# Three moves in a hybrid decoder layer: the samples' mask load, the splits before the SSD branch projection, and the evictions of the output projection

## The chip, the cores and the metric

One core of a Trainium2 chip runs the whole program in one launch. The metric is device time in microseconds (us) of that core. Engines are named as in the profile: PE is TensorE's matmul, PEld its weight load, DVE is VectorE, ACT ScalarE, POOL GpSimd, and SP (SyncE) issues most transfers. L12 is line 12 of the kernel before.

## The reference, cut to what matters

One layer is computed for two groups that share the weights: a prompt of 256 tokens and 8 samples of 8 tokens, each with 2048 cached positions. Together they are 320 columns.

```
x = x + 0.5 * SwiGLU1(RMSNorm(x))
h = RMSNorm(x); P = h @ w_in_proj            # z, xBC, dt | q, k/v x 3, gates | merge gates
y_ssd = mamba_mixer(...)                     # conv, chunked scan, SiLU(z) gate, group norm of 4 x 512
y_nsa = sparse attention over compressed, selected and window rows of the cache
m = sig(gA) * (y_ssd @ w_branch_ssm) + sig(gB) * (y_nsa @ w_branch_attn)
x = x + m @ w_out
x = x + 0.5 * SwiGLU2(RMSNorm(x))
```

In the samples' window branch the 8 new keys of a sample are masked: key n is hidden from a query at t < n. That mask is the input wm, 128 x 8 numbers.

## The kernel before, in words

**Dense units.** All big products run through `dense` (L335). A unit is one output tile of 128 rows and 320 columns. Weights come from DRAM in blocks of 128 x 1024 f32 (512 KB) through three raw buffers. Each block is split into a high half `wh`, cast on ACT (`w_hi`, L317), and a lower half `wl`, a subtraction on DVE (`w_lo`, L326). The input is split the same way into `xh` and `xl`, by `split`: a cast on ACT (L261), then a subtraction on DVE (L264). For each of the k tiles PE runs three matmuls (L345 to L347), wh with xh, wh with xl, wl with xh, so 24 a unit at 8 tiles. Splitting is two units ahead of PE: at the start of a unit `w_hi` is issued for the unit two further on, after the third k tile `w_lo`, and `w_lo` ends by asking SP for the next raw block (L308), which waits until this DVE instruction has freed its buffer. wh and wl have three buffers each, the PSUM tiles of the units (tag pd) three.

**Side work.** Everything that is not a dense unit is written as generators in a scheduler S. After each k tile `S.tick()` runs: callbacks given to `S.defer(n, f)` fire after 2n ticks, then the generators get a step whenever a credit, filled at a rate set for each stage, reaches one. `S.step()` takes one step by hand. Engines work in order, and each queue holds its instructions as the program issues them.

**The samples' side work.** `ssd()` runs two generators mixed: `prompt_chunks` and `sample_chunks`. The first ends by taking `early_bias(2)`, a generator that loads the bias table in 16 pieces of 64 KB on SP, two a step (L1440), and, in a last step of its own, the mask `wb` (L1444); then `early_kv`, which loads the first three key/value tiles. A tile is four pages of 256 KB, two issued by SP and two by POOL (L1431), or one 1 MB window read by SP (L1427). `sample_attn` follows. Its first DVE instruction adds a part of the bias to the mask (L1458), so it needs both. Then it asks for four more tiles (a ring of seven, one of them in the tail of `xbc`) and goes through 40 tiles. One step transposes one tile's weights on PE (L1512; copied by ACT, L1514), in three steps of five computes scores for one or two tiles ahead (PE L1481 and L1486, maxima on DVE L1494, exponentials on ACT L1505), multiplies with the values (L1526), and does a part of the combine (L1541 to L1572). A tile is asked for, by a deferral of two ticks, after the step that used the tile seven before it. During this the dense units are those of z (L2016, L2017 gate them; squares and their sums for the group norm, L368, L373, L396) and then of the SSD branch.

**The SSD branch.** For each half h of the 16 input tiles, a loop splits eight tiles of xbc into yh and yl; then `NST` = 2 steps are taken by hand; then eight units follow.

**The output projection.** For each of eight units m: the eviction adds half of the product to x2 on DVE (L2073), scales it by the norm's weights (L416, DVE), splits that into hh and hl (L261, L264), squares x2 on ACT (L368) and gathers the squares on POOL, the last on DVE (L373). FFN 2 (`ffn`) then takes hh and hl as its input; its first unit needs all eight of them, in order.

```
for k in range(8):                                   # SSD branch, each half
    split(yh[:, k, :], yl[:, k, :], xbc[:, 8 * h + k, :])
for _ in range(NST):
    S.step()
for m in range(8):                                   # output projection
    p = bank("pd", (128, NT))
    dense(wo[m], mh, ml, p)
    v.scalar_tensor_tensor(x2[:, m, :], p, 0.5, x2[:, m, :], op0=ALU.mult, op1=ALU.add)
    norm_pre(x2, m, P_N2, hh, hl)
    sq.add(x2[:, m, :])
```

Of the kernel before, what the change touches and what calls it, by code (L numbers as in the profile page):

```python
# [10 lines left out]
F32 = mybir.dt.float32  # L11
# [4 lines left out]
ALU = mybir.AluOpType  # L16
# [22 lines left out]
P_N1, P_NM, P_N2, P_CW, P_CB, P_SN, P_DS, P_QN, P_DTB, P_AL, P_PE, P_W2, P_QR = (  # L39
    0, 8, 16, 24, 120, 144, 160, 176, 180, 181, 182, 214, 342)  # L40
# [67 lines left out]
NST = 2  # L108
# [89 lines left out]
def step_kernel(ctx, tc, I, O):  # L198
    nc = tc.nc
    pe, v, a, g, sp = nc.tensor, nc.vector, nc.scalar, nc.gpsimd, nc.sync  # L200
    ctx.enter_context(tc.manual_schedule())
    S = Sched()
# [8 lines left out]
    def bank(tag, shape=(128, 512)):  # L211
        bufs = dict(pd=3, sc=2, pt=2, po=1)[tag]
        t = ps.tile([128, 512], F32, tag=tag, bufs=bufs, name=f"ps_{tag}")[: shape[0], : int(np.prod(shape[1:]))]
        if len(shape) == 3:
            t = t.rearrange("p (a b) -> p a b", a=shape[1])
        elif len(shape) == 4:
            t = t.rearrange("p (a b c) -> p a b c", a=shape[1], b=shape[2])
        return t
# [39 lines left out]
    def split(hi, lo, src, eh="a"):  # L258

        if eh == "a":  # L260
            a.copy(hi, src)  # L261
        else:
            gcopy(hi, src)
        v.tensor_tensor(lo, src, hi, op=ALU.subtract)  # L264
# [35 lines left out]
    st = dict(load=0, split=0, raw={}, hl={})  # L300
# [34 lines left out]
    def dense(unit, xh, xl, out, cut=1, extra=None):  # L335

        k0, K = 0, sum(n for _, n in unit)
        for i, n in unit:
            w_ready(i + SA - 1)
            wh, wl = st["hl"].pop(i)  # L340
            w_hi()
            for k in range(n):
                s = slice(128 * k, 128 * k + 128)
                kk = k0 + k
                pe.matmul(out, wh[:, s], xh[:, kk, :], start=kk == 0, stop=False)  # L345
                pe.matmul(out, wh[:, s], xl[:, kk, :], start=False, stop=False)  # L346
                pe.matmul(out, wl[:, s], xh[:, kk, :], start=False, stop=kk == K - 1)  # L347
                if extra:
                    extra()
                if k == 2:  # L350
                    w_lo()
                if (kk + 1) % cut == 0:
                    S.tick()
            k0 += n
# [58 lines left out]
    def norm_pre(x, k, gcol, hh, hl):  # L413

        h = tp.tile([128, NT], F32, tag="hf", name="hf")
        v.tensor_scalar(h, x[:, k, :], par[:, gcol + k : gcol + k + 1], None, op0=ALU.mult)  # L416
        split(hh[:, k, :], hl[:, k, :], h)

    def norm_scale(sq, pool):

        rsb = pool.tile([128, NT], F32, name="rsb")
        rs = tp.tile([128, 3], F32, tag="nrs", bufs=1, name="nrs")

        def spread():
            bc = bank("pt", (128, NT))
            spread_rows(bc, rs)
            a.copy(rsb, bc)

        S.defer(sq.delay + 1, lambda: sq.roots(rs))
        S.defer(sq.delay + 6, spread)  # L430
        return rsb
# [351 lines left out]
    hh = hp_.tile([128, 8, NT], F32R, tag="hh", name="hh")  # L783
    hl = hp_.tile([128, 8, NT], F32R, tag="hl", name="hl")
# [16 lines left out]
    sq = Squares(8, 6)  # L801
# [4 lines left out]
    sq = Squares(8)  # L806
# [11 lines left out]
    hh = hp_.tile([128, 8, NT], F32R, tag="hh", name="hh")  # L818
    hl = hp_.tile([128, 8, NT], F32R, tag="hl", name="hl")
# [613 lines left out]
    def early_bias(n):  # L1433
        pl = right.enter_context(tc.tile_pool(name="sb", bufs=1, side="right"))
        st["bias"] = pl.tile([128, PAST], F32, name="bias")
        for i in range(2 * T):
            t, s = divmod(i, 2)
            src = bass.AP(tensor=tr0.tensor, offset=tr0.offset + (16 * TL + 512) * s + 7 - t,
                          ap=[[TL, 16], [1024, 2], [1, 512]])
            sp.dma_start(st["bias"][t :: T, :].rearrange("p (c s n) -> p c s n", c=2, s=2)[:, :, s, :], src)  # L1440
            if i % n == n - 1:
                yield
        st["wb"] = pl.tile([128, 8], F32, name="wb")
        sp.dma_start(st["wb"], I["wm"])  # L1444
        yield

    def early_kv():
        pl = right.enter_context(tc.tile_pool(name="sk", bufs=1, side="right"))
# [167 lines left out]
    def ssd():  # L1616
# [118 lines left out]
        def prompt_chunks():  # L1735
# [9 lines left out]
            for i, (q, c) in enumerate(items):  # L1745
                if i + 1 < 8:
                    if c:
                        yield from until(("x", q + 1))
                    stage_a(*items[i + 1])
                yield  # L1750
                if i + 1 < 8:
                    decay(*items[i + 1])
                stage_b(q, c)
                yield
                if i + 2 < 8:
                    load_ab(*items[i + 2])
                state(q, c)
                if c:
                    ready["y", q] += 1
                if i + 1 < 8:  # L1760
                    weigh(*items[i + 1])
                if c and q < 3:
                    load_ecb(q + 1)
                yield
                store("outS")
                if i == EB:
                    yield from until("conv")
                    late = early_bias(2)
                if i >= EB:
                    next(late, None)  # L1770
# [149 lines left out]
    p = bank("pd", (128, NT))  # L1920
# [12 lines left out]
    for i in range(12):  # L1933
        p = bank("pd", (128, NT))
# [11 lines left out]
    for i in range(4):  # L1946
        p = bank("pd", (128, NT))
# [14 lines left out]
    for i in range(4):  # L1962
        p = bank("pd", (128, NT))
# [12 lines left out]
    for n, i in enumerate(XBC_RUN):  # L1976
        p = bank("pd", (128, NT))
# [14 lines left out]
    for i in range(16):  # L1992
        p = bank("pd", (128, NT))
# [32 lines left out]
    for i in range(16):  # L2026
        if i % 4 == 0:
            force(lambda: ready["y", i // 4] == 2)
            sq = Squares(4, fold=True)
        p = bank("pd", (128, NT))  # L2030
# [3 lines left out]
    for h in range(2):  # L2034
        if h:
            S.flush()
        yh = hp_.tile([128, 8, NT], F32R, tag="hh", name="yh")
        yl = hp_.tile([128, 8, NT], F32R, tag="hl", name="yl")
        for k in range(8):
            split(yh[:, k, :], yl[:, k, :], xbc[:, 8 * h + k, :])  # L2040
        for _ in range(NST):
            S.step()
        for m in range(8):
            p = bank("pd", (128, NT))
            dense(wbs[h][m], yh, yl, p)
            if h == 0:
                a.copy(xbc[:, m, :], p)
            else:
                v.tensor_tensor(xbc[:, m, :], xbc[:, m, :], p, op=ALU.add)
                v.scalar_tensor_tensor(mg[:, m, :], mg[:, m, :], 1.0, xbc[:, m, :], op0=ALU.add, op1=ALU.mult)  # L2050
# [4 lines left out]
    so, x2, oh_, ol_ = (st[k] for k in ("so", "x2", "oh", "ol"))  # L2055
    mhl = hp_.tile([128, 16, NT], F32R, tag="Ax", name="mhl")
    mh, ml = mhl[:, 0:8, :], mhl[:, 8:16, :]
    for m in range(8):
        p = bank("pd", (128, NT))
# [7 lines left out]
    sq = Squares(8, 5, True)  # L2067
    hh = hp_.tile([128, 8, NT], F32R, tag="hh", name="hh")
    hl = hp_.tile([128, 8, NT], F32R, tag="hl", name="hl")
    for m in range(8):  # L2070
        p = bank("pd", (128, NT))
        dense(wo[m], mh, ml, p)
        v.scalar_tensor_tensor(x2[:, m, :], p, 0.5, x2[:, m, :], op0=ALU.mult, op1=ALU.add)  # L2073
        norm_pre(x2, m, P_N2, hh, hl)
        sq.add(x2[:, m, :])
    rsb = norm_scale(sq, so)

    def evac2(m, p):
# [155 lines left out]
```

## Time and profile before

| | |
|---|---|
| median of 3 runs (lowest, highest) | 1316.9 us (1314.0, 1320.02) |
| the profiled execution | 1319.28 us |
| its span, first to last instruction | 1317.6 us |
| mean granted TensorE clock | 0.981 of 2.4 GHz |
| busy: PE, PEld, DVE, ACT, POOL | 96%, 87%, 67%, 45%, 26% |
| transfers | 251.67 MB, mean 191 GB/s |

Times inside the profile count from the first instruction. A busy PE is one with matmuls in flight, whatever its clock; PEclk is the clock that was granted, 1.00 for 2.4 GHz and 0.50 for 1.2 GHz, and a stretch with both shows a mean. The releaser in square brackets of a row is inferred; an engine named there that had long been done stands for another, often a transfer.

### The profile page before, as it was taken

To read this page: it belongs to the slowest core of one execution; us is meant where nothing else is said; L and a number is where in the kernel's file an instruction comes from. 1 tells how busy PE (TensorE), PEld (TensorE's weight loads), DVE (VectorE), ACT (ScalarE), POOL (GpSimd) and SP (SyncE) were. 2 spreads that over 40 slices of the span, in tenths; PEclk is the share of its full clock that TensorE was granted. 3 is DMA by queue.
4 is the path that set the end of the run, shared out by engine and by line. 5 is a ranking of instruction groups with operands and counts; after the bars stand their busy time and mean duration, and the time that the engine had idled before them with its cause. 6 is when DMAs were issued, how large, how long until landed. Compare 5 with 4: busy or idle time off the path is not lost. (4 is left out here: it accounts for less than half of the span.)

```text
span 1317.6 us, 28585 instructions
## 1 busy us (share of the span) xinstructions
PE 1260.2 (96%) x10779; PEld 1151.3 (87%) x10779; DVE 877.1 (67%) x1872; ACT 590.5 (45%) x1149; POOL 347.0 (26%) x567
## 2 busy tenths in 40 slices
PE   8999999999999998889999998898999999999998
PEld 8999999999988888777897777775769999999998
DVE  5576666655586577976568888777678665656542
ACT  4444444444455334446664442455564343333322
POOL 2233221232200335655335664121210010000000
PEclk9899999999999998999999999898999999999999
DMA  8466666766663445521167876998974444444553
GB/s 275 146 215 213 206 197 197 233 202 221 203 195 121 138 147 212 189 69 50 65 207 236 269 228 194 325 339 289 331 284 154 152 145 135 146 154 150 153 163 92
DMA packets 102212, 251.67 MB, mean 191 GB/s; under 512 B 14648, under 2 KB 41273, under 8 KB 100121
## 3 DMA queue, kind: packets, MB, share of 16 engines
q1 hardware_dynamic: 89722, 213.44, 49.1%
q0 software_dynamic: 12352, 36.40, 8.4%
q8 instruction: 85, 1.39, 0.4%
q14 instruction: 53, 0.43, 0.1%
HBM read 235.07 MB, written 23.10 MB: 196 GB/s over the span
## 5 line engine op out<-in xcount | busy, mean ns | idle before, releaser
L345 PE MATMUL ps_pd<-hh,wh 128*128 128x320 f32 x1320 | 440.9, 334 | 2.9 <-ACT hh L261 1.8
L326 DVE TENSOR_TENSOR wl<-wraw,wh 128x1024 fp32r<-128x1024 f32 (+1 forms) x245 | 303.2, 1239 | 178.0 <-ACT wh L317 172.2
L346 PE MATMUL ps_pd<-hl,wh 128*128 128x320 f32 x1320 | 413.8, 314 | 1.3 <-DVE hl L454 1.1
L347 PE MATMUL ps_pd<-hh,wl 128*128 128x320 f32 x1320 | 413.7, 313 | 1.2 <-DVE wl L326 1.1
L317 ACT CAST wh<-wraw 128x1024 fp32r<-128x1024 f32 (+1 forms) x245 | 252.1, 1031 | 139.1 <-PE ps_pd L346 99.8
L345 PEld LDWEIGHTS ps_pd<-hh,wh 128*128 128x128 f32 x1320 | 253.2, 192 | 22.0 <-issue 11.4
L346 PEld LDWEIGHTS ps_pd<-hl,wh 128*128 128x128 f32 x1320 | 253.6, 192 | 9.5 <-issue 4.8
L347 PEld LDWEIGHTS ps_pd<-hh,wl 128*128 128x128 f32 x1320 | 253.0, 192 | 2.0 <-DVE wl L326 2.0
L345 PE MATMUL ps_pd<-ah,wh 128*128 128x320 f32 x352 | 109.4, 311 | 0.0
L347 PE MATMUL ps_pd<-ah,wl 128*128 128x320 f32 x352 | 108.9, 309 | 0.0
L580 DVE TENSOR_TENSOR pgl<-pg,pgh 128x512 fp32r<-128x512 f32 x128 | 82.5, 685 | 29.6 <-ACT pgh L573 29.3
L346 PE MATMUL ps_pd<-al,wh 128*128 128x320 f32 x320 | 98.8, 309 | 0.0
L568 POOL DMA_DIRECT2D pg<-in_cache x136 | 74.2, 546 | 83.6 <-DVE pgl L580 42.3
L238 POOL TENSOR_SCALAR ah<-ff 128x320 fp32r<-128x320 f32 x44 | 20.1, 457 | 275.0 <-DVE ff L482 275.0
L477 ACT ACTIVATE sg<-sg 128x320 f32<-128x320 f32 x44 | 20.8, 472 | 127.1 <-DVE sg L476 127.1
L573 ACT CAST pgh<-pg 128x512 fp32r<-128x512 f32 x128 | 72.7, 616 | 10.0 <-PE ps_sc L714 8.0
L713 PE MATMUL ps_sc<-pgh,w1h 128*128 128x256 f32 x256 | 68.5, 288 | 1.3 <-ACT pgh L573 1.3
L714 PE MATMUL ps_sc<-pgh,w1l 128*128 128x256 f32 x256 | 68.2, 288 | 0.0
L345 PEld LDWEIGHTS ps_pd<-ah,wh 128*128 128x128 f32 x352 | 66.2, 188 | 0.4
L347 PEld LDWEIGHTS ps_pd<-ah,wl 128*128 128x128 f32 x352 | 66.1, 188 | 0.0
L346 PEld LDWEIGHTS ps_pd<-al,wh 128*128 128x128 f32 x320 | 60.2, 188 | 0.0
L1431 POOL DMA_DIRECT2D KV<-in_cache x54 | 29.1, 539 | 109.4 <-PE ps_po L1526 90.6
(476 smaller groups left out, 2207.5 us busy)
## 6 DMA issues: line engine op xcount, KB each, us to landing
wraw<-in_wproj SPq DMA_DIRECT2D x77, 512.0 KB
wraw<-in_w1in SPq DMA_DIRECT2D x44, 512.0 KB
wraw<-in_w2in SPq DMA_DIRECT2D x44, 512.0 KB
pg<-in_cache POOLq DMA_DIRECT2D x136, 128.0 KB, 4.0
pg<-in_cache SPq DMA_DIRECT2D x120, 128.0 KB
KV<-in_cache POOLq DMA_DIRECT2D x54, 256.0 KB, 5.9
KV<-in_cache SPq DMA_DIRECT2D x54, 256.0 KB
wraw<-in_w1out SPq DMA_DIRECT2D x16, 512.0 KB
```

Of the source, the lines that this page charges most:

```text
L317: a.copy(h[:, :n], st["raw"][i][:, :n])
L326: v.tensor_tensor(l[:, :n], st["raw"].pop(i)[:, :n], st["hl"][i][0][:, :n], op=ALU.subtract)
L345: pe.matmul(out, wh[:, s], xh[:, kk, :], start=kk == 0, stop=False)
L346: pe.matmul(out, wh[:, s], xl[:, kk, :], start=False, stop=False)
L347: pe.matmul(out, wl[:, s], xh[:, kk, :], start=False, stop=kk == K - 1)
L477: a.activation(s, s, AF.Silu)
L568: e.dma_start(page(s, half)[:, i, :], I["cache"][ds(r, 1), :, 256 * c : 256 * c + 256].rearrange("o p f -> p (o f)"))
L573: a.copy(h[:, 8 * half : 8 * half + 8, :], page(s, half)[:, :, 64 * q : 64 * q + 64])
L580: v.tensor_tensor(l[:, 8 * half : 8 * half + 8, :], page(s, half)[:, :, 64 * q : 64 * q + 64], h[:, 8 * half : 8 * half + 8, :], op=ALU.su ...
L713: pe.matmul(ph, wh[:, j, :], h[:, :, j, :], start=q + j == 0, stop=False)
L714: pe.matmul(ph, wl[:, j, :], h[:, :, j, :], start=False, stop=False)
L1431: e.dma_start(t[:, j, :], I["cache"][ds(r, 1), :, 512:1024].rearrange("o p f -> p (o f)"))
```

## The change

Three edits. `early_bias` asks for the mask first, ahead of all bias pieces and in the same step as the first two, and has no step of its own for it any more. In the SSD branch the two steps by hand are taken after the second and after the fifth of the eight splits. In the output projection the evictions of units 0 to 6 are deferred by three ticks, to the third k tile of the next unit, behind that tile's `w_lo`; the last one stays where it is.

```diff
     def early_bias(n):
         pl = right.enter_context(tc.tile_pool(name="sb", bufs=1, side="right"))
         st["bias"] = pl.tile([128, PAST], F32, name="bias")
+        st["wb"] = pl.tile([128, 8], F32, name="wb")
+        sp.dma_start(st["wb"], I["wm"])
         for i in range(2 * T):
...
             if i % n == n - 1:
                 yield
-        st["wb"] = pl.tile([128, 8], F32, name="wb")
-        sp.dma_start(st["wb"], I["wm"])
-        yield
...
         for k in range(8):
             split(yh[:, k, :], yl[:, k, :], xbc[:, 8 * h + k, :])
-        for _ in range(NST):
-            S.step()
+            if k in (1, 4):
+                S.step()
...
         dense(wo[m], mh, ml, p)
-        v.scalar_tensor_tensor(x2[:, m, :], p, 0.5, x2[:, m, :], op0=ALU.mult, op1=ALU.add)
-        norm_pre(x2, m, P_N2, hh, hl)
-        sq.add(x2[:, m, :])
+
+        def evac(m=m, p=p):
+            v.scalar_tensor_tensor(x2[:, m, :], p, 0.5, x2[:, m, :], op0=ALU.mult, op1=ALU.add)
+            norm_pre(x2, m, P_N2, hh, hl)
+            sq.add(x2[:, m, :])
+
+        if m < 7:
+            S.defer(1.5, evac)
+        else:
+            evac()
```

## Rows read from the trace of the kernel before

**Rows 1.** The page's first part: busy time, share of the span and instructions of each engine.

```profile
PE 1260.2 (96%) x10779; PEld 1151.3 (87%) x10779; DVE 877.1 (67%) x1872; ACT 590.5 (45%) x1149; POOL 347.0 (26%) x567
```

**Rows 2.** PE's waits between 795 and 1100 us: the waiting instruction, its inferred releaser, us in total, times, longest.

```profile
PE ps_pt L396 <- DVE ncol L401: 3.6, 1, 3.6
PE ps_sc L1481 <- DVE yl L264: 3.1, 2, 2.5
PE ps_sc L1838 <- DVE h L1840: 2.3, 1, 2.3
PE ps_sc L1481 <- DMA KV<-in_cache: 2.3, 2, 1.2
PE ps_pd L345 <- ACT hh L261: 1.8, 1, 1.8
```

**Rows 3.** Windows: the stretch in us, its length, busy us of each engine (instructions), granted clock, DMA share, GB/s.

```profile
800.00:810.00 10.00, 7.66 (x35) 5.47 (x34) 8.92 (x12) 1.84 (x3) 4.82 (x5) 0.83 0.54 184
...
835.00:840.00 5.00, 5.00 (x20) 4.97 (x21) 3.31 (x17) 0.14 (x2) 2.00 (x4) 0.50 1.05 404
840.00:845.00 5.00, 5.00 (x47) 2.04 (x46) 2.57 (x7) 1.94 (x5) 0.00 (x0) 0.92 1.01 395
930.00:940.00 10.00, 8.91 (x122) 5.41 (x114) 6.45 (x26) 4.18 (x10) 2.15 (x4) 1.00 0.85 280
1080.00:1090.00 10.00, 9.19 (x51) 8.94 (x52) 6.86 (x21) 3.77 (x5) 0.00 (x0) 0.83 0.48 158
845.00:985.00 140.00, 134.45 (x1974) 95.60 (x1976) 98.60 (x373) 81.02 (x186) 27.96 (x52) 0.98 0.88 314
```

**Rows 4.** SP's queue in order of time: start, us of issue, transfer, how many.

```profile
822.40 1.18 SPq L1440 DMA_DIRECT2D bias<-trev  x2
823.63 0.85 SPq L1444 DMA_DIRECT2D wb<-in_wm  x1
824.58 1.69 SPq L308 DMA_DIRECT2D wraw<-in_wproj  x1
...
827.85 4.75 SPq L1431 DMA_DIRECT2D KV<-in_cache  x6
```

**Rows 5.** The chain of work that ended last, in order of time: start, us, what. The last bias piece's issue and the mask's transfer.

```profile
822.99 0.59 SPq L1440
...
823.63 8.43 DMA wb<-in_wm
```

**Rows 6.** DVE in order of time: start, us, line, operation, shapes, how many; in brackets the idle time before it and its releaser.

```profile
832.14 0.17 DVE L1458 TENSOR_TENSOR wb<-wb,bias 128x8 f32<-128x8 f32 x1 [3.01 <-DMA wb<-in_wm]
...
833.15 1.22 DVE L326 TENSOR_TENSOR wl<-wraw,wh 128x1024 fp32r<-128x1024 f32 x1
834.28 0.48 DVE L373 TENSOR_TENSOR sqa<-sqa,sq 128x320 f32<-128x320 f32 x1
```

**Rows 7.** ACT in order of time: the high half before that lower half.

```profile
830.22 1.05 ACT L317 CAST wh<-wraw 128x1024 fp32r<-128x1024 f32 x1 [1.73 <-DMA wraw<-in_wproj]
```

**Rows 8.** PE in order of time, at the first half's splits: the scores of two tiles, and the first matmul of the branch.

```profile
900.93 1.02 PE L1481 MATMUL ps_sc<-xbc,qbs 64*32 64x512 f32 x2 [2.53 <-DVE yl L264]
903.19 1.03 PE L1481 MATMUL ps_sc<-KV,qbs 64*32 64x512 f32 x1 [1.24 <-DMA KV<-in_cache]
...
907.05 0.64 PE L345 MATMUL ps_pd<-yh,wh 128*128 128x320 f32 x1
```

**Rows 9.** SP's queue: the issue of the tile that lies in xbc.

```profile
893.00 0.92 SPq L1431 DMA_DIRECT2D xbc<-in_cache  x2
```

**Rows 10.** DVE there: the first of the second step's two maxima, and the last instruction of its combine.

```profile
905.72 0.69 DVE L1494 CUSTOM_DVE_ANT_0 P<-ps_sc,bias 128x512 f32<-128x512 f32 x1 [3.02 <-PE ps_sc L1486]
...
908.04 1.06 DVE L1572 TENSOR_REDUCE ocs<-R 128x64 f32<-128x512 f32 x1
```

**Rows 11.** ACT there: the second step's last exponential.

```profile
908.23 0.71 ACT L1505 ACTIVATE P<-P,ms 128x512 f32<-128x512 f32 x1
```

**Rows 12.** DVE in the output projection: lower half, the first eviction, its lower half of hl, the next unit's lower half; and the last eviction.

```profile
1050.91 1.23 DVE L326 TENSOR_TENSOR wl<-wraw,wh 128x1024 fp32r<-128x1024 f32 x1 [0.46 <-ACT wh L317]
1052.05 0.48 DVE L2073 SCALAR_TENSOR_TENSOR x<-ps_pd,x 128x320 f32<-128x320 f32 x1
...
1053.48 0.49 DVE L264 TENSOR_TENSOR hl<-hf,hh 128x320 fp32r<-128x320 f32 x1 [0.53 <-ACT hh L261]
1054.79 1.22 DVE L326 TENSOR_TENSOR wl<-wraw,wh 128x1024 fp32r<-128x1024 f32 x1 [0.82 <-ACT wh L317]
...
1079.25 0.48 DVE L2073 SCALAR_TENSOR_TENSOR x<-ps_pd,x 128x320 f32<-128x320 f32 x1
```

**Rows 13.** ACT there: the first eviction's cast, and the next high half.

```profile
1052.99 0.46 ACT L261 CAST hh<-hf 128x320 fp32r<-128x320 f32 x1 [2.11 <-DVE hf L416]
...
1053.73 1.03 ACT L317 CAST wh<-wraw 128x1024 fp32r<-128x1024 f32 x1
```

**Rows 14.** PE at the start of FFN 2: the wait for the last hh, and two matmuls in a row.

```profile
1080.70 0.41 PE L345 MATMUL ps_pd<-hh,wh 128*128 128x320 f32 x1 [1.82 <-ACT hh L261]
...
1081.62 0.31 PE L345 MATMUL ps_pd<-hh,wh 128*128 128x320 f32 x1
1081.77 0.31 PE L346 MATMUL ps_pd<-hl,wh 128*128 128x320 f32 x1
```

## The prediction

> **What bounds the kernel now.** The first view is busy time by engine: TensorE (PE) is busy 96% of the span [rows 1]. So the end moves only if PE's idle time shrinks, if its clock sits at 1.2 GHz for less time, or if new waits are put before it. The second view is PE's waits in the stretch that holds all three edits [rows 2]. The five longest come to 13 us: 3.6 us for a sum of squares, 3.1 us (2.5 and 0.6) at the samples' scores put down to the split (yl), 2.3 us (1.2 and 1.1) there for KV tiles, 1.8 us for hh at the start of FFN 2, and 2.3 us for h, which no edit touches. The third view is the windows [rows 3]. After the 2.3 us wait for h the clock averages 0.83 over 10 us, which is 10 x 0.17 x 2 = 3.4 us at 1.2 GHz. After the 3.6 us wait it is 0.50 for 5 us and 0.92 for the next 5, 5 + 0.8 = 5.8 us at least. After the 1.8 us wait it is 0.83 over 10 us, 3.4 us. Around the KV wait of 1.1 us it stays at 1.00. Half-rate time t costs t/2 of PE's work, so a long wait costs more than its idle time.
>
> The profiled execution took 1319.28 us (span 1317.6, 1.7 around it); the median of the three runs is 1316.9, 2.4 below it. I work out a gain against the first and take it off the median. A measurement of this kernel can tell about 0.5% (6.6 us) from no change.
>
> **Edit 1, the mask.** SyncE (SP) issues the last pair of bias pieces at 822.40 and the mask at 823.63 [rows 4]. The mask is only 4 KB, but it lands 8.43 us later, because it queues behind all that was issued before it [rows 5]. DVE's L1458 needs it and the bias, and stands idle 3.01 us until 832.14 [rows 6]. Everything on DVE behind L1458 is late by as much: the gating of the z unit, the weights' lower half at 833.15, and at 834.28 the sum for which PE waits. With the mask asked for ahead of all bias pieces, what is late next? First the bias: its last piece is issued 0.64 us ahead of the mask (822.99 to 823.63) on the same queue [rows 5]. If it takes as long, DVE gains 0.64; if it has landed by the time DVE arrives, the full 3.01. Second the weights: ACT's high half waits for its own transfer and starts at 830.22 [rows 7]. It ends at 831.3, and the lower half follows it, so at most 833.15 - 831.3 = 1.85 us is gained. L1458 also comes a step earlier in DVE's order and may now wait ahead of one gather like that at 834.28, 0.48 us, which takes the lower bound to 0.2. Bounds 0.2 to 1.85; I take 1.4, nearer the upper, since the bias pieces are ahead of the mask's 128 tiny packets.
>
> PE then resumes at 833.5 instead of 834.9, an idle time of 2.2 instead of 3.6. The nearest wait is the one of 2.3 us, with 3.4 us at half rate. Before, PE did 5.9 / 2 = 2.95 us of full-rate work from 834.9 to 840.8. Now it does 1.7 in 3.4 us and the other 1.25 at full rate, done at 838.15: gain 2.65. If the half-rate time stays as long, the gain is the bare 1.4. I take 2.6 for the edit.
>
> What it costs: one mask issue (0.85 us) stands ahead of the first bias pair, and what covers it is that nothing reads the bias before L1458, eight steps later: nothing, and 0.85 us for SP's weight loads without that cover. The generator also has one step fewer. So the three early KV loads, each two SP and two POOL transfers, come a step earlier. POOL has nothing else in its queue there. On SP the first one's SP half (512 KB) now stands ahead of the weight load at 824.58. Six such transfers take SP 4.75 us to issue [rows 4], so this load leaves 2 x 0.79 - 0.85 = 0.7 us later, with 512 KB ahead of it: at 395 to 404 GB/s [rows 3] another 1.3 us. It feeds a split that DVE reaches a dense unit later, 3.5 us of PE's work. With that cover the price is nothing; without it, 2 us.
>
> All sample steps also run one step earlier against the dense units, so at each split it is the next tile's step that falls there. That can move KV waits either way; the nearest rows are those waits themselves, 2.5 and 1.2 us [rows 8]. Price 0, bounds -3.7 to +3.7.
>
> **Edit 2, the splits.** No PE instruction lies among the eight splits; the steps' matmuls come after them in PE's order already. The wait at 900.93 is put down to yl, yet the score matmul L1481 reads a KV tile (kept in xbc) and qbs, not yl [rows 8]. SP issued that tile at 893.00 to 893.92 [rows 9], so it would have landed after 7.0 us, against 8.43 for the mask. I read 900.93 as a landing, and the next wait, 903.19, is named as one. So moving steps between splits takes off nothing: the scores wait for KV in either order. It can cost: the splits left for after the second step now stand behind its maxima and its combine on DVE (905.72 to 909.1) [rows 10] and its exponentials on ACT (to 908.9) [rows 11]. PE starts the first unit at 907.05 and wants split 5 after fifteen matmuls of 0.147 us, 2.2 us at full rate, so at 909.3; splits come every 0.4 us from about 909.2 with lower halves 0.5 later. Price 0.3 us for both halves together; bounds -0.5 (ACT's transposed copies start earlier) and +2.
>
> **Edit 3, the output projection.** DVE and ACT run one loop per unit: lower half 1050.91, eviction 1052.05, next lower half 1054.79 [rows 12]; cast 1052.99, and behind it and the square the next high half 1053.73 [rows 13]. The period is 3.88 us, where PE needs 24 matmuls of 0.147 us (1081.62 to 1081.77) [rows 14], 3.53. So the evictions fall behind by 0.35 a unit, and the last one (1079.25) makes PE wait for hh. Putting eviction m behind the split of unit m+1 does not break this loop: the order around it, high half, lower half, eviction, cast, square, high half, is the same, and ACT must still pass each cast before the next high half. It saves only the first eviction's place, where two splits now run back to back: high half 1 as soon as PE has left unit 0 (about 1051.1, where 1053.73 stood), lower half 1 at 1052.1 behind lower half 0, eviction 0 at 1053.3, high half 2 at 1055.0, and from there 3.88 a unit: high half 7 at 1074.4, eviction 6 at 1074.4 + 1.06 + 1.14 = 1076.6. Eviction 7 follows it directly on DVE, behind its lower half (1053.48 + 0.49 - 1052.05 = 1.9): 1078.45 instead of 1079.25. Gain 0.8; bounds 0 (the loop slips back) and 1.8 (no wait left). hh then comes at 1079.9, not 1080.70. The wait shrinks from 1.8 to about 1.05, nearest to that of 1.1 which left the clock at full. So I also take off half of the 3.4 us at half rate, 1.7. Edit 3: 2.5, or 0.8 if the clock drops all the same.
>
> **Sum.** 2.6 - 0.3 + 2.5 = 4.8 us: 1314.5 for the profiled execution, 1312.1 for the median.
>
> **A rule against it.** The mask's row shows 8.43 us in a busy queue [rows 5]. The Trainium skill, "DMA: Bandwidth & Descriptors", section "Anatomy of one DMA — SWDGE (gpsimd) path", fits a transfer (of the other issuing path) as some 2 us plus its bytes over the peak rate. By that the mask was in place before DVE asked and the wait was for something else: edit 1 is worth nothing and the sum is 2.2. The row speaks against it here; it is the third rival.
>
> **Rivals.**
> 1. Forecast, 0.42: gains of 3 to 7 us.
> 2. Given back to KV, 0.20. The stage of the samples runs with DMA at 0.88 of its time [rows 3], and PE stands there for tiles. If the landings at 903 and 938 don't move, the 2.6 of edit 1 turns into longer waits: 1314.7. For: both waits. Against: KV loads are released by PE's own progress, so they should shift with it.
> 3. The mask was not the last to come, 0.10. The bias, or another transfer, holds L1458 as long: 1314.7 too, by edit 3 alone.
> 4. The step shift helps, 0.20. The scores fall in the first of the two steps at the split with their tiles asked for a step sooner; some 2.5 of the 3.7 us goes, and 1.7 of half rate: 1312.1 - 4.2 = 1308.
> 5. Slower, 0.08: the late splits starve PE. If the tiles are in time, PE reaches the first unit straight away, while splits wait for maxima and exponentials (two of 0.7 us each) that wait for PE's scores. That is some 3 us at each half, plus 1.7 of clock: 2 x 4.7 = 9.4, so 1312.1 + 9.4 = 1321.5. It decides once a half loses over 2.4 us, and passes 0.5% only if edit 1 fails as well.
>
> **Numbers.** Likeliest 1312.1. Range 1307 to 1318.5: below, rival 4 with the longer DVE gain; above, no gain and part of rival 5. Under 1310.3 lie rival 4 and a little of the forecast, 0.26; over 1323.5 the tail of rival 5, 0.04; 0.70 within.
>
> **What would show it.** Right: L1458 idle about 1.5 us or less and not on the mask; PE's wait for the sum about 2.2; half rate after it shorter; eviction period still 3.88 in the middle, the last one at about 0.8 us nearer to its unit; the wait for hh near 1 us and the clock at 1.00 after it; score waits at the splits still there. Wrong: a period of 3.5, no DVE wait at L1458 at all, or a score wait at the split that vanishes with KV landing as before.

## The result: 0.54% slower, lost among the samples' key/value tiles

| | before | after |
|---|---|---|
| median | 1318.55 us (8 runs) | 1326.6 us (8 runs) |
| profiled execution, its span | 1319.28, 1317.6 us | 1328.19, 1326.5 us |
| ratio, 95% interval | | 1.0054 [1.0032, 1.0076] |

On 1318.5 us the ratio is +7.1 us, interval 4.2 to 10.0. The forecast was a gain of 4.8 us, and no rival came as high: the slowest stood at 1321.5. Busy time and PE's waits from 795 to 1110 us, as in [rows 1, 2]; lines behind the diff have moved by one or two, so L1480 is the scores (L1481 before):

```profile
PE 1269.7 (96%) x10779; PEld 1155.8 (87%) x10779; DVE 877.7 (66%) x1872; ACT 590.1 (44%) x1149; POOL 346.7 (26%) x567
```

```profile
PE ps_sc L1480 <- DMA KV<-in_cache: 6.6, 3, 3.6
PE ps_pt L396 <- DVE sqa L373: 3.1, 2, 2.1
...
PE ps_sc L1480 <- DMA KV<-in_cwin: 1.7, 1, 1.7
PE ps_pt L396 <- DVE ncol L401: 1.6, 1, 1.6
PE ps_sc L1480 <- DMA xbc<-in_cache: 1.5, 1, 1.5
PE ps_pd L345 <- ACT hh L261: 1.0, 1, 1.0
```

Over the whole span PE is idle as long as before (1326.5 - 1269.7 = 56.8 us, and 57.4), but busy 9.5 us longer with the same instructions, at a mean granted clock of 0.976 for 0.981. So part of the loss is clock, as the stages below show.

The two waits that edits 1 and 3 aimed at shrank: the sum (ncol) from 3.6 to 1.6, hh from 1.8 to 1.0. Larger are the score waits on tiles, 6.6 + 1.7 + 1.5 = 9.8 us in five waits, where before had 5.4 with those put down to yl, and the wait for sqa, 3.1 for 1.0. PE's rows show where the shorter sum, four of the five tile waits and the longer wait for sqa lie (start, us, idle before and its releaser):

```profile
831.77 0.78 PE L396 MATMUL ps_pt<-ones,sqa 128*128 128x1 f32 x6 [1.64 <-DVE ncol L401]
884.14 1.85 PE L1480 MATMUL ps_sc<-KV,qbs 64*32 64x512 f32 x14 [3.58 <-DMA KV<-in_cache]
914.67 0.94 PE L396 MATMUL ps_pt<-ones,sqa 128*128 128x1 f32 x6 [2.10 <-DVE sqa L373]
952.23 1.06 PE L1480 MATMUL ps_sc<-KV,qbs 64*32 64x512 f32 x8 [1.69 <-DMA KV<-in_cwin]
958.70 0.59 PE L1480 MATMUL ps_sc<-xbc,qbs 64*32 64x512 f32 x1 [1.45 <-DMA xbc<-in_cache]
982.38 1.12 PE L1480 MATMUL ps_sc<-KV,qbs 64*32 64x512 f32 x14 [1.95 <-DMA KV<-in_cache]
```

Tiles are asked for and scored in order, eight L1480 each, so counting names them: 13 at 884.14, 18 (1.06 us) at 903.23, 29 (a window) at 952.23, 31 at 958.70, 36 at 982.38 (some of the expectations below call this last one 37). The windows, columns as in [rows 3]:

```profile
835.00:840.00 5.00, 5.00 (x45) 2.23 (x44) 3.82 (x10) 1.88 (x5) 1.50 (x3) 0.85 1.03 410
840.00:845.00 5.00, 5.00 (x39) 4.15 (x32) 3.04 (x9) 3.47 (x9) 0.00 (x0) 1.00 1.03 386
960.00:970.00 10.00, 10.00 (x114) 7.44 (x113) 2.77 (x16) 4.15 (x8) 1.07 (x2) 0.69 0.73 257
980.00:990.00 10.00, 8.05 (x78) 5.41 (x80) 2.77 (x16) 1.83 (x6) 0.00 (x0) 0.67 0.93 333
845.00:985.00 140.00, 128.17 (x1806) 88.89 (x1810) 88.23 (x338) 69.86 (x161) 27.95 (x52) 0.95 0.86 298
1090.00:1100.00 10.00, 8.92 (x60) 8.30 (x59) 7.30 (x21) 3.80 (x6) 0.41 (x1) 1.00 0.39 122
```

From the sum (834.91 before, 831.77 after) to the first matmul on oh_ (1019.32, 1030.30) it takes 198.5 us instead of 184.4. Of these 14.1 us, 10.5 lie in the 140 us of the long window: PE is busy 6.3 us less (134.45 to 128.17), and the clock averages 0.95, not 0.98, both rounded, another 140 x 0.03 = 4.2 us or so of full-rate work [rows 3]. The rest lies at its ends and isn't itemised. The wait of 2.10 us at 914.67, with half rate behind it until 919, belongs to this loss but is on no tile. It is 1.49 and 1.47 us in two of the runs below whose steps also run early, before lacks it, and what causes it is not shown. Against the 14.1 us stand 3.1 us won where PE resumes at the sum (1.2 of them were there already at 798) and 2.1 us in FFN 2: 14.1 - 3.1 - 2.1 = 8.9, the difference of the spans.

What happened to tile 13 is seen in two queues. Its two halves are asked for by SP and by POOL. SP's rows, after and then before (872 to 877 us: start, us of issue):

```profile
874.52 0.34 SPq L308 DMA_DIRECT2D wraw<-in_wbs  x1
875.65 1.61 SPq L1431 DMA_DIRECT2D KV<-in_cache  x2
```

```profile
873.69 0.34 SPq L308 DMA_DIRECT2D wraw<-in_wbs  x1
874.82 0.93 SPq L1431 DMA_DIRECT2D KV<-in_cache  x2
```

POOL's half of the same tile, after and before:

```profile
868.48 1.20 POOL L1431 DMA_DIRECT2D KV<-in_cache  x2 [3.09 <-PE ps_po L1525]
```

```profile
873.89 1.20 POOL L1431 DMA_DIRECT2D KV<-in_cache  x2 [2.77 <-PE ps_po L1526]
```

And SP's wait in that stretch (864 to 876), after and before:

```profile
SPq L308 <- DVE wl L326: 7.3, 1, 7.3
```

```profile
SPq L308 <- DVE wl L326: 2.9, 1, 2.9
```

POOL's half follows PE, and with PE 3.1 us ahead and the steps moved it came 5.4 us earlier. SP's half stands behind a weight load, which stands still until DVE has split an older block; that is tied to the dense units, which did not move by a step. So it came 0.8 us later than before, 7.2 us behind its sister. PE, before, scored the pair at 883.85, 9.0 us after SP's issue:

```profile
883.85 1.09 PE L1481 MATMUL ps_sc<-KV,qbs 64*32 64x512 f32 x16
```

After the change it got there at 884.14 - 3.58 = 880.56, 4.9 us after the issue, and stood until 8.5 us after it.

Tile 31 shows the same, SP behind a weight load and POOL 4.9 us earlier:

```profile
949.86 0.34 SPq L308 DMA_DIRECT2D wraw<-in_wbs  x1
950.99 0.92 SPq L1431 DMA_DIRECT2D xbc<-in_cache  x2
```

```profile
946.05 1.20 POOL L1431 DMA_DIRECT2D xbc<-in_cache  x2 [3.34 <-PE ps_po L1525]
```

At tile 36 the lag is 4.3 us. Tile 18's halves are 0.5 us apart, and window 29 has one part alone, issued 0.5 us behind a weight load; for these two the rows name no more than the landing.

### The profile page after: what moved, and what is told of

The parts are those of the page before. It is cut to its first block, busy times and chain, and to the rows that moved or that the text cites. A ratio compares the mean times of both kernels' runs of the same rounds, so it can differ in the third digit from the quotient of the medians.

```text
span 1326.5 us, 28582 instructions
## 1 busy us (share of the span) xinstructions
PE 1269.7 (96%) x10779; PEld 1155.8 (87%) x10779; DVE 877.7 (66%) x1872; ACT 590.1 (44%) x1149; POOL 346.7 (26%) x567
## 5 line engine op out<-in xcount | busy, mean ns | idle before, releaser
L345 PEld LDWEIGHTS ps_pd<-hh,wh 128*128 128x128 f32 x1320 | 252.5, 191 | 21.3 <-issue 11.5
```

## The experiments

Each was compared with the kernel before on the same chip; us are the ratio on 1318.5, with its 95% interval. Theories and rivals are numbered here as in the expectations; theory 1 is that the lost step put key/value requests behind waiting weight loads on SP's queue. A profile is one execution, and its span can lie several us from the median of its kernel, so a wait in a single profile is no mean.

**All three edits, the step put back.**

```diff
             if i % n == n - 1:
                 yield
+        yield
```

> All three edits, but with the step of its own that stood at the end of the bias generator put back (an empty step), so that every sample step falls on the same place of the dense units as before. Theory 1 (the lost step put KV requests behind waiting weight loads on SP's queue): the score waits for tiles 13, 29, 31 and 37 go, the forecast of 4 to 5 us comes back, 1312 to 1315 us, 0.3 to 0.5% under before. Rival 2 (the steps between the splits cost it, whatever the phase): it stays slower than before by 5 to 9 us. Rival 3 (the mask's earlier issue delays weights or KV): also slower, by 5 to 9.

Ratio 1.0000 [0.9976, 1.0024]: 0 us, -3.2 to +3.2. The 7 us are gone, so rivals 2 and 3 are out at the 5 to 9 us that they named: with all three edits in and the mask first, the time is that of before. But the gain forecast did not come either; the interval excludes 4 to 5 us. PE's score waits, and that for the sum:

```profile
PE ps_sc L1481 <- DMA xbc<-in_cache: 3.9, 2, 2.4
PE ps_sc L1481 <- DMA KV<-in_cache: 1.6, 2, 1.4
PE ps_pt L396 <- DVE ncol L401: 0.8, 1, 0.8
```

One of them is new, at tile 3, where neither before nor the change has one:

```profile
838.70 1.03 PE L1481 MATMUL ps_sc<-xbc,qbs 64*32 64x512 f32 x1 [1.55 <-DMA xbc<-in_cache]
```

Before waited 3.6 us for the sum and then ran 5.9 us at half rate. Here PE waits 0.8 for the sum and stays at full rate, but then waits 1.55 for this tile and runs about 6.8 us at half rate. In this profile most of what the sum gained is given back there, as the prediction's rival 2 says.

**Each edit alone.** The first as in the change (diff above, its first two parts), the second, and the third.

> The first edit alone, as in the change (mask asked for first, its own step gone). Theory 1: slower than before by 5 to 10 us, with PE waits for KV at the scores that before does not have, 6 us or more in all. Rival 2 (the splits): faster by about 3 us. A third possibility, that it takes the shift and the moved steps together: within 3 us of before.

> The second edit alone. Theory 1: within 1.5 us of before (my 0.3 us of the forecast), KV waits as before. Rival 2: slower by 5 to 9 us. If part of the loss is the wait of 2.1 us for the sum of squares behind the first half's steps, that wait shows here too and it costs 2 to 4 us.

> The third edit alone. Forecast and theory 1: faster by 2 to 2.5 us, loop period 3.88 us, PE's wait for hh near 1.0 us instead of 1.8, clock 1.00 behind it. A rival (that gain was the rest's): no difference, within 1 us.

The mask with its lost step: 1.0074 [1.0053, 1.0095], +9.8 us (7.0 to 12.5), the whole loss by itself, with waits of 2.96, 1.72, 1.49 and 2.01 us at tiles 13, 29, 31 and 36. The splits: 0.9994 [0.9977, 1.0011], -0.8 us (-3.0 to +1.5), without the wait of 2.1 us for sqa that the expectation looked for. The evictions: 0.9988 [0.9969, 1.0007], -1.6 us (-4.1 to +0.9), which neither shows nor denies the 2 to 2.5 us; the profile has PE's wait for hh at 1.0 and 1.00 of the clock behind it.

**The step alone, the mask's place alone.** The first is the kernel before with this; the second has the mask first, as in the change, and keeps the step.

```diff
         st["wb"] = pl.tile([128, 8], F32, name="wb")
         sp.dma_start(st["wb"], I["wm"])
-        yield
```

> The kernel before with only the empty step taken out: the mask stays the last of the load, behind all bias pieces, and every sample step falls one step earlier against the dense units. Theory 1 (the phase of the steps decides): slower than before by 6 to 10 us, with the score waits for tiles 13, 29, 31 and 37 as after the change. Rival 3 (it is the mask's place that costs): within 1.5 us of before.

> The mask asked for first, the empty step kept, nothing else changed. Forecast: faster by 2.6 us, PE's wait for the sum near 2 us or under instead of 3.6. Rival of the prediction (given back to KV): PE gets to the scores earlier, but the waits for KV there grow by as much and the time is within 1 us of before.

Without the step: 1.0050 [1.0021, 1.0079], +6.6 us (2.8 to 10.4), though nothing else was touched and the mask is still last. PE's score waits there, and DVE's wait for the mask:

```profile
PE ps_sc L1480 <- DMA KV<-in_cache: 2.9, 2, 1.5
PE ps_sc L1480 <- DMA KV<-in_cwin: 1.8, 1, 1.8
PE ps_sc L1480 <- DMA xbc<-in_cache: 1.4, 1, 1.4
```

```profile
832.44 0.17 DVE L1457 TENSOR_TENSOR wb<-wb,bias 128x8 f32<-128x8 f32 x1 [2.54 <-DMA wb<-in_wm]
```

Here it is tiles 16, 29, 31 and 36, each the first behind a weight load on SP, but at 16 the two halves are asked for within 0.2 us of each other; 13 and 18 were in time. Tile 13 shows that the order on SP is not the whole account: its SP half came 7.2 us behind POOL's here too, and PE scored the pair without a wait, 4.5 us after that request, where the change waited until 8.5 us after it. SP's, POOL's and PE's rows:

```profile
881.62 1.23 SPq L1431 DMA_DIRECT2D KV<-in_cache  x2
```

```profile
874.45 1.20 POOL L1431 DMA_DIRECT2D KV<-in_cache  x2 [3.09 <-PE ps_po L1525]
```

```profile
886.14 1.23 PE L1480 MATMUL ps_sc<-KV,qbs 64*32 64x512 f32 x16
```

Why the same transfer took up to 8.5 us in one and at most about 4.5 in the other is open.

The mask first with the step kept: 0.9981 [0.9962, 1.0000], -2.5 us (-5.0 to 0.0), at the forecast's 2.6, though the interval touches no gain. DVE's addition to the mask, which waited 3.01 us before, waits 1.28 us there and 1.02 in the change, neither put down to the mask:

```profile
832.26 0.17 DVE L1458 TENSOR_TENSOR wb<-wb,bias 128x8 f32<-128x8 f32 x1 [1.28 <-DMA xbc<-in_cache]
```

```profile
828.60 0.17 DVE L1457 TENSOR_TENSOR wb<-wb,bias 128x8 f32<-128x8 f32 x1 [1.02 <-DMA xbc<-in_cache]
```

**Key/value transfers off SP's queue.**

```diff
-    def load_kv(i, engines=(g, sp, g, sp)):
+    def load_kv(i, engines=(g, g, g, g)):
...
-            sp.dma_start(t, I["cwin"][b].rearrange("p (t f) -> p t f", t=4))
+            g.dma_start(t, I["cwin"][b].rearrange("p (t f) -> p t f", t=4))
```

> The changed kernel with all key/value transfers (four pages a tile, and the windows) issued by POOL, so that none stands behind a weight load on SP's queue, nor a weight load behind them. Theory 1: the score waits of 1.5 us and more for tiles 13, 29, 31 and 37 go, and it gains 7 to 10 us, 1317 to 1320 us or less. Rival 4 (the transfers come late because the rate of the transfers bounds the stage): the waits stay, and it stays within 3 us of the change, 1324 to 1330. Against both: POOL issues two more pages a tile, 1.2 us each time in the trace, which delays each tile by about 1 us.

> The same issue by POOL on the version with all three edits and the empty step kept. Theory 1: with no key/value request behind a weight load the phase of the steps no longer matters, so it comes within 3 us of the kernel with the step gone, and 0 to 4 us under its own version with SP halves (1318). Rival 4: the two keep their 9 us of difference.

> The kernel before with all key/value transfers issued by POOL and none of the three edits. Theory 1: before too pays for tiles behind weight loads (waits of 1.2 and 1.1 us named as such, 2.5 read as such), so 1 to 5 us faster, 1313 to 1317. Against the version with all three edits and the step kept (1311.6) it tells what the edits are worth where the transfers do not take it back: forecast 4.8 us, so 1316.4; if the mask's gain goes into later waits even so, 2 us, 1313.6.

On the change: 0.9984 [0.9962, 1.0007], -2.1 us (-5.0 to +0.9) against before, so 9.2 us better than the change itself. On the version with the step kept: 0.9951 [0.9928, 0.9974], -6.5 us (-9.5 to -3.4). On before: 0.9985 [0.9968, 1.0002], -2.0 us (-4.2 to +0.3). The same bytes at the same places of the program, and the loss is gone: the rate of the transfers (rival 4) did not bound the stage. In the version with the step kept, the stretch of the samples runs at the full clock, with DMA at the same 0.88 of its time as before:

```profile
845.00:985.00 140.00, 136.07 (x2101) 98.35 (x2102) 103.84 (x401) 82.17 (x190) 59.66 (x111) 1.00 0.88 310
```

Phase still tells the two apart by 4.3 us (0.9984 - 0.9951), with some 4.2 either way: more than the 3 expected, under the 7.1 with SP's halves, and hardly clear of nothing. PE's longest score wait, for tile 38, is 2.62 us in the one and 1.44 in the other. The three edits are worth 6.5 - 2.0 = 4.5 us here, with some 3.8 either way: the forecast's size, where SP's order doesn't take it back.

**Five late tiles, five neighbours.** The second run has (12, 17, 24, 30, 35) in both places.

```diff
         t = KV[i] = ring[i % NKV]
+        if i in (13, 18, 29, 31, 36):
+            engines = (g, g, g, g)
...
-            sp.dma_start(t, I["cwin"][b].rearrange("p (t f) -> p t f", t=4))
+            (g if i in (13, 18, 29, 31, 36) else sp).dma_start(t, I["cwin"][b].rearrange("p (t f) -> p t f", t=4))
```

> The changed kernel with five of the 40 tiles alone (13, 18, 29, 31, 36: those whose scores PE waited for) issued wholly by POOL; the other 35 as before, halves on SP and POOL. Theory 1 (their SP halves stood behind a weight load that was waiting for its buffer): the waits of 3.6, 1.1, 1.7, 1.5 and 2.0 us at these five shrink to under 0.7 each, and 6 to 10 us of the change's loss comes back: 1316 to 1320 us. Rival 5 (POOL issue helped because SP had less to do as a whole): at most a fifth of the gain of the full POOL version, 1 to 3 us, 1323 to 1326.

> A control: the changed kernel with five neighbours (tiles 12, 17, 24, 30, 35: the other tile of the same pair, or the window before) issued wholly by POOL, and the five late ones left as in the change. Theory 1: the late ones still stand behind the same weight loads; the waits stay within 1 us of what they were, and the time within 3 us of the change, 1324 to 1330. Rival 5: as good as the five late tiles, within 2 us of that run.

The late five: 0.9967 [0.9950, 0.9985], -4.4 us (-6.6 to -2.0), so 11.5 better than the change, from five of 40 tiles. All of tile 13 is asked for at 866.47, and PE's scores of it don't wait:

```profile
866.47 2.55 POOL L1433 DMA_DIRECT2D KV<-in_cache  x4 [3.09 <-PE ps_po L1527]
```

```profile
878.73 1.09 PE L1482 MATMUL ps_sc<-KV,qbs 64*32 64x512 f32 x16
```

None of the five waits is left; the longest at the scores is now 1.16 us, at tile 38. The neighbours: 1.0022 [0.9999, 1.0045], +2.9 us (-0.1 to +5.9), 4.2 better than the change with some 4.2 either way, where at most 3 was expected. Of the five waits three stay, that of tile 31 at half its length:

```profile
950.65 1.06 PE L1482 MATMUL ps_sc<-KV,qbs 64*32 64x512 f32 x8 [1.82 <-DMA KV<-in_cwin]
956.43 0.59 PE L1482 MATMUL ps_sc<-xbc,qbs 64*32 64x512 f32 x1 [0.77 <-DVE wl L326]
976.79 0.66 PE L1482 MATMUL ps_sc<-KV,qbs 64*32 64x512 f32 x7 [1.67 <-DMA KV<-in_cache]
```

So the waits at 13 and 18 are gone, which theory 1 did not expect, and tile 11 waits 1.55 us instead (876.30), its SP half 3.2 us behind POOL's and behind a weight load. Which tiles it is matters, 7.3 us between the two sets with some 3.8 either way. Less on SP's queue may help by itself too (rival 5 in part); 4.2 us with that interval don't settle it.

**The phase set by hand.**

```diff
-W0, W1, W2, W3, WS, EB = 3, 3, 6, 1, 4, 2
+W0, W1, W2, W3, WS, EB = 3, 3, 6, 1, 5, 2
```

> The changed kernel with one more empty step between the requests of the first tiles and the first scores (five for four): the three early tiles are still asked for a step earlier, as in the change, but scores, values and the requests of all later tiles fall about where they did before. Theory 1: the waits for tiles 13 and 29 go, and 5 to 9 us of the loss comes back, 1317 to 1321. Rival 6 (it is the earlier request of the first tiles, ahead of a weight load, that costs): it stays at 1324 to 1329.

0.9929 [0.9908, 0.9949]: 1310.7 us, -9.4 us (-12.1 to -6.7) against before and 16 less than the change. It beats both kernels, by one more empty step, and by 6 us more than expected. The waits for tiles 13 and 29 are gone; tile 18 waits 1.86 us (902.32). Tile 13's pair is scored without a wait, when before scored it, and SP asks for the pair behind the weight load from 9.2 us ahead of that on:

```profile
873.66 0.34 SPq L308 DMA_DIRECT2D wraw<-in_wbs  x1
874.79 2.64 SPq L1431 DMA_DIRECT2D KV<-in_cache  x4
```

```profile
883.99 1.54 PE L1480 MATMUL ps_sc<-KV,qbs 64*32 64x512 f32 x16
```

The earlier request of the first three tiles is innocent (rival 6). Why this is 9 us under the version with the step put back, whose steps fall almost alike, stays open. Their profiles can't tell, for the spans are 1312.5 and 1311.9: the first is the slowest of its six executions, the second one of the fastest of its twelve.

## Why the prediction was wrong, point by point

**The step that failed** is the last one of edit 1: "All sample steps also run one step earlier against the dense units ... Price 0, bounds -3.7 to +3.7." It cost 6.6 us alone (2.8 to 10.4), 7.1 with all three edits in (1.0054 against 1.0000) and 12.3 with the mask first (1.0074 against 0.9981), each of these two with some 4 either way, and decided the sign. I had looked at the waits that were there [rows 8] and bounded the shift by them. A moved step doesn't only lengthen or shorten those; it can make other tiles late whose request lands behind a weight load, and there are as many candidates as tiles. The largest new wait, 3.58 us, was at tile 13, which did not wait before. The row to bound it was among SP's waits, in the trace of before from 845 to 1000 us:

```profile
SPq L308 <- DVE wl L326: 74.2, 16, 11.1
```

For half of that stretch SP stands before a weight load, up to 11.1 us at a time, and a key/value request behind it stands as long. I priced SP's queue only for the first load, at 824 us. Such a request is not always late enough to be waited for (tile 13 without the step), so this row names the candidates and not the cost.

**The sentence against the prediction's rival 2**, that "KV loads are released by PE's own progress, so they should shift with it", is true for POOL's halves (868.48 for 873.89) and false for SP's (875.65 for 874.82).

**Edit 1's own part** held. DVE's wait fell from 3.01 to 1.02, no longer on the mask; PE's wait for the sum to 1.64, where 2.2 was said; the stretch at half rate shortened as forecast, 0.85 and 1.00 where 0.50 and 0.92 stood [rows 3]. That this pair fell by 2.0 and not by 1.4 is in part chance: over all the profiles PE's wait for the sum averages 3.0 us in the five with the mask last and 1.7 in the nine with it first, about the 1.4 forecast. With the transfers on SP and the step kept, the mask alone was worth 2.5 us (0.0 to 5.0).

By the Trainium skill's fit of some 2 us plus bytes ("DMA: Bandwidth & Descriptors", section "Anatomy of one DMA — SWDGE (gpsimd) path"), which is given for the other issuing path, the mask would have been there. With the mask last the wait is put down to it in four of the five profiles, 2.51 to 3.01 us, and in the fifth, the splits alone, to another transfer, 1.12 us; with the mask first it never is. So the traces speak against that fit for a small transfer behind a full queue.

**Edit 2** did nothing measurable (-0.8 us, -3.0 to +1.5), as said, and the reading of the wait "yl" as a landing was right: with the step kept the same wait is put down to the tile itself:

```profile
898.50 1.01 PE L1481 MATMUL ps_sc<-xbc,qbs 64*32 64x512 f32 x2 [2.38 <-DMA xbc<-in_cache]
```

My rival for slower, splits that starve PE, was the wrong mechanism: PE waited 0.35 us for them.

**Edit 3** went by its steps: two splits back to back, then the period of 3.88 us as in [rows 12], the last eviction, 27.57 us after the first lower half where before had 28.34 (0.77 nearer, 0.8 was said), the wait for hh, and 1.00 of the clock behind it (1090 to 1100) where 0.83 stood. DVE, and PE's row:

```profile
1061.90 2.48 DVE L326 TENSOR_TENSOR wl<-wraw,wh 128x1024 fp32r<-128x1024 f32 x2 [0.46 <-ACT wh L317]
...
1067.05 1.23 DVE L326 TENSOR_TENSOR wl<-wraw,wh 128x1024 fp32r<-128x1024 f32 x1 [0.82 <-ACT wh L317]
...
1070.94 1.23 DVE L326 TENSOR_TENSOR wl<-wraw,wh 128x1024 fp32r<-128x1024 f32 x1 [0.82 <-ACT wh L317]
...
1089.47 0.48 DVE L2074 SCALAR_TENSOR_TENSOR x<-ps_pd,x 128x320 f32<-128x320 f32 x1
```

```profile
1091.14 0.41 PE L345 MATMUL ps_pd<-hh,wh 128*128 128x320 f32 x1 [0.97 <-ACT hh L261]
```

From FFN 2's first matmul (1086.62, 1075.63 before) to the end it is 239.9 us, 242.0 before: 2.1 less, of 2.5 forecast. In the medians it can't be told from nothing.

**The sum without the shift** was 4.8. Measured together with the step kept it is 0 (-3.2 to +3.2), so that failed too, by less; with the transfers on POOL it is 4.5 (some 3.8 either way). That fits "given back to KV", and the wait at tile 3 with the step kept is such a place; but the three edits measured apart (the mask with the step kept, the splits, the evictions) add up to -4.9 us, with some 4.2 either way, so the runs don't settle it.

## What to carry to other kernels

A step taken out of a schedule moves everything behind it against the rest; before pricing that, list which instructions of each in-order queue end up behind one that waits for another engine. Two halves of a transfer on two queues are as late as the later one. Where the phase is arbitrary, try the neighbouring phases: the empty step put in before the first scores was worth 16 us against the change, over three times the gain the three edits were forecast to bring, and the one put back behind the bias load 7.

## What the runs showed of the hardware that was not expected

POOL asked for four pages in 2.55 us (two in 1.20), and asking for all 40 tiles raised its busy time in the 140 us from 27.96 us before to 59.66 with the step kept; PE's busy time in that stretch was higher all the same, 136.07 for 134.45 us.

The length of one wait did not decide the granted clock. With the transfers on POOL and the step kept, waits of 1.34 us (896.67) and 1.44 us (970.80) left it at 1.00, and with the five neighbours on POOL so did 1.82 us (950.65). But there 1.67 us (976.79) left 0.85 and 0.80 over the two stretches of 5 us from 975 on. In the change, the wait of 1.95 us at 982.38 left 0.67 over 980 to 990 us, and 1.69 and 1.45 us, ending 6.5 us apart, left 0.69 over 960 to 970; it fell only after the second.
